# Expert weights in double tiles: 16 KB in a row on a partition where one is free, 8 KB otherwise

## The chip, the core and the metric

The kernel runs on one core of a Trainium2 chip. It is measured in microseconds (us) of device time for one execution; the median of three runs before the change is 1324.52 us (1322.39 to 1326.03). The engines are TensorE (PE; PEld is its weight load), VectorE (DVE), ScalarE (ACT), GpSimd (POOL) and SyncE (SP), which here issues nearly all loads. 16 DMA engines move the data; a packet is what one of them carries in one piece.

## The reference, cut to what matters

One layer of a diffusion model over 512 tokens of 1024 channels: adaLN modulation from a conditioning vector (`w_mod`), an input projection into attention, Hyena and Conformer branches, an output projection with a residual, and then 16 experts. Every expert takes the 64 tokens with the highest affinity. Everything is float32. What the change is about is the expert part:

```
aff = softmax(h @ w_router);  gate, idx = top_k(aff.T, 64)       # per expert
xe = h[idx]                                                     # 16 x 64 x 1024
a = einsum('ecd,edf->ecf', xe, w1);  u = einsum('ecd,edf->ecf', xe, w3)   # f: 2048
y = einsum('ecf,efd->ecd', silu(a) * u, w2) * gate
x = rmsnorm(x + g2 * zeros.at[idx].add(y), final_norm_g)
```

w1, w3 and w2 are 8 MB per expert each, 24 MB together and 384 MB for all 16. (MB here is 1,048,576 bytes.)

## The kernel before, in words

**Tiles.** Large data lies in 24 equal tiles of 128 partitions x 8 KB (1 MB each) of one pool: weights on their way, their split halves, activations, attention tables, the reloaded rows of x, the accumulator. `U` (L65) hands one out and counts it; `free` and `free_only` (L76, L80) take back a number of tiles, without naming them.

**Loads.** All loads are put into a list in the order of their use (L227 to L268) and are issued from SP. `pump(keep)` (L72) issues from the head of the list for as long as more than `keep` tiles are left by the count; `free` calls it. `take` (L166) hands over a loaded tile, and issues up to it where it isn't loaded yet. The keep values (`ADA_KEEP` L489, `PK` L734) hold tiles back for the work that comes next. A load waits on SP until its tile's last readers are done, and SP works through its queue in order. SP also waits for an earlier load of its own before it issues the next; some 8 are under way at a time.

**Channels.** An expert's w1 and w3 come in 8 blocks each of 128 rows (channels), one row of 8 KB per partition: block k holds channels 128k to 128k + 127. w2 comes in 8 blocks of 256 rows, two rows of 4 KB per partition. Each of these loads reads 1 MB that lies in one piece in memory. The activations must have the same channel on the same partition: x is transposed in blocks of 128 neighbouring columns (L1012, L1168, L1193), and the hidden activations are transposed for w2 with a column step of 2 (L1339), because a partition holds two neighbouring rows.

**Order of the work.** First filters, projections, convolution (to some 250 us), then attention and output projection with routing, in an order that is written out by hand for TensorE (L1103): S, T, A are steps of the attention, r the routing of a block of tokens, d a part of the last adaLN group (`adaln(3)`, four loads of `w_mod`), f the release of two tiles. `best` (L1077) finds the top tokens on DVE. Then comes the expert loop (L1300): for each of the 8 blocks it takes w1 and w3, runs 4 pairs of matmuls (L1313 and L1314, w1 and w3, each on one half of the array) and frees both tiles; every matmul shows as two in the records, so that a block has 8 pairs there. Between the blocks lie the scatter of the expert before (L1205, L1208) and the gather of the next one's rows (L1185, L1193). Then 16 transposes of the hidden activations (L1340), and 8 blocks of w2 with 4 pairs in the records each (L1353). After the last expert the accumulated rows are stored from SP (L1364), and the rows that the last expert changes are written again from POOL (L1381).

Of the kernel before, what the change touches and what calls it, by code (L numbers as in the profile page):

```python
# [25 lines left out]
NU = 24  # L26
# [24 lines left out]
def hybrid_kernel(ctx: ExitStack, tc: tile.TileContext, a, out: bass.AP):  # L51
    nc = tc.nc
    small = ctx.enter_context(tc.tile_pool(name="small", bufs=1))
    big = ctx.enter_context(tc.tile_pool(name="big", bufs=NU))
# [6 lines left out]
    used = [0]  # L61
    ready = {}
    limit = [12]

    def U(name, dt=FT):  # L65
        used[0] += 1
        assert used[0] <= NU, name
        return big.tile([128, 2048], dt, name=name, tag="U")
# [3 lines left out]
    def pump(keep=0):  # L72
        while loads and loads[0] is not None and used[0] < NU - keep and len(ready) < limit[0]:
            loads.popleft()()

    def free(k=1, keep=0):  # L76
        used[0] -= k
        pump(keep)

    def free_only(k=1):  # L80
        used[0] -= k
# [84 lines left out]
    def take(key):  # L166
        while key not in ready:
            assert loads and used[0] < NU, key
            go = loads.popleft()
            if go is not None:  # L170
                go()
        return ready.pop(key)
# [11 lines left out]
    def load_xr(i):  # L184
        def go():
            t = U("ld")
            for h in range(2):
                nc.sync.dma_start(t[:, h * D:(h + 1) * D], by_col(a["x"])[2 * i + h])
            ready["xr", i] = t
        loads.append(go)  # L190
# [61 lines left out]
    for u in (1, 0):  # L252
        for n in range(2):
            load(("wo", n, u), a["w_out"][u * 512:(u + 1) * 512, n * 512:(n + 1) * 512].rearrange("(k p) n -> p k n", p=128),
                 v512)
            if u and not n:
                load_xr(0)
                load_xr(1)
    for e in range(E):
        for k in range(8):  # L260
            if e == 0 and k == 6:
                for q in range(4):
                    load_wm(3, q)
            load(("w1", e, k), a["w1"][e, k * 128:(k + 1) * 128, :])
            load(("w3", e, k), a["w3"][e, k * 128:(k + 1) * 128, :])
        for j in range(8):

            load(("w2", e, j), a["w2"][e, j * 256:(j + 1) * 256].rearrange("(p k) n -> p (k n)", k=2))  # L268
# [46 lines left out]
    fw3s = [U("fw3s", FR) for _ in range(2)]  # L315
# [13 lines left out]
    free_only(1)  # L329
    xn = [take(("x", 0)), take(("x", 1))]  # L330
    ss = stat[:, 4:8]
    hr = [U("hr0"), U("hr1")]
# [16 lines left out]
    def x_transposed():  # L349
        yield from transpose_rows([half(xn[b // 2], b % 2) for b in range(4)], 4,  # L350
                                  lambda k4, b: v512(hr[k4]).rearrange("p k (c r) -> p k r c", r=8)[:, :, 2 * b:2 * b + 2])
        free_only(2)
# [3 lines left out]
    def filt_out():  # L356
        sd.extend([U("sm"), U("df")])
# [16 lines left out]
        free_only(4)  # L374
# [8 lines left out]
    def spectrum():  # L383

        sm, df = sd
        dft = v512(take("dft"))
        K.extend([U("KE"), U("KP"), U("KM")])
# [24 lines left out]
        free_only(3)  # L412


    def adaln(g):
# [10 lines left out]
        for k in range(8):  # L426
            if k % per == 0:
                w = take(("wm", g, k // per)).rearrange("p (k j n) -> p k j n", k=per, n=512)
# [3 lines left out]
            if k % per == per - 1:  # L432
                free_only(1)
                pump(ADA_KEEP[g])
                yield
# [16 lines left out]
        for blk in range(4):  # L452
            c = slice(blk * 128, (blk + 1) * 128)
            if ncol == 4:
                nc.tensor.transpose(p[:, c], row[:, c], ident)
# [33 lines left out]
    ADA_KEEP = [7, 4, 2, 0]  # L489
# [3 lines left out]

    def modulate_split(src, n, v, name, pool="01010101"):

        nu = (8 * n) // 2048
        hi = [U(name + "h", FR) for _ in range(nu)]
        lo = [U(name + "l", FR) for _ in range(nu)]
# [11 lines left out]
    def split(raw, keep, dve=()):  # L510
        hi = U("wh", FR)
        lo = U("wl", FR)
# [4 lines left out]
        free(1, keep)  # L517
# [26 lines left out]
    free_only(2)  # L544
# [9 lines left out]
    def mix_alloc(i):  # L554
        mixh[i] = U(f"mixh{i}", FR)
        mixl[i] = U(f"mixl{i}", FR)
# [8 lines left out]
    glt, yc = [], []  # L565
# [5 lines left out]
    def evac_cf(m, ps):  # L571
# [3 lines left out]
        else:  # L575
            if m == 0:

                glu = U("glu")
                glt.extend(glu[:, i * 544:i * 544 + 542] for i in range(2))
# [15 lines left out]
    def ln_cf():  # L595
# [27 lines left out]
        free_only(1)  # L623
# [6 lines left out]
    def evac_hy(i, ps):  # L630
        if i == 0:
            hx[0] = U("hx")
        if i == 4:
            hx[1] = U("hz")
# [8 lines left out]
    def hyena():  # L643
# [8 lines left out]
        for o in range(2):  # L652
# [59 lines left out]
            free_only(1)  # L712
        free_only(6)
# [7 lines left out]
    def evac_q(m, ps):  # L721
        if m == 0:
            Q.append(v512(U("Q")))
# [10 lines left out]
    PK = [6, 7, 3, 5, 8, 2]  # L734

    def project(c, ntile, evac, order=None, ctx_part=None):
# [5 lines left out]
        parts = []  # L742
# [734 lines left out]
```

## Time and profile before

| | |
|---|---|
| Median of 3 runs | 1324.52 us |
| Profiled execution, its time | 1322.8 us |
| Its span (first to last instruction) | 1321.0 us |
| PE busy | 1249.0 us (95%) |
| DVE, ACT, POOL busy | 39%, 17%, 12% |
| Moved by DMA | 457.99 MB (of 10^6 bytes), in 72979 packets |
| Expert loads | 384 of 1 MB, 19.9 us from issue to landing (median) |

The page divides the span into 40 slices of 33 us, and gives each engine's busy share there in tenths. The chain of waits goes back from the last instruction and names, at each step, what released it. Matmuls overlap in the records, so that a busy PE need not be at its peak, and a DMA share can come out a little above 1.

### The profile page before, as it was taken

To read this page: it belongs to the slowest core of one execution; us is meant where nothing else is said; L and a number is where in the kernel's file an instruction comes from. 1 tells how busy PE (TensorE), PEld (TensorE's weight loads), DVE (VectorE), ACT (ScalarE), POOL (GpSimd) and SP (SyncE) were. 2 spreads that over 40 slices of the span, in tenths; PEclk is the share of its full clock that TensorE was granted. 3 is DMA by queue.
4 is the path that set the end of the run, shared out by engine and by line. 5 is a ranking of instruction groups with operands and counts; after the bars stand their busy time and mean duration, and the time that the engine had idled before them with its cause. 6 is when DMAs were issued, how large, how long until landed. Compare 5 with 4: busy or idle time off the path is not lost.

```text
span 1321.0 us, 14776 instructions
## 1 busy us (share of the span) xinstructions
PE 1249.0 (95%) x5914; PEld 566.4 (43%) x5914; DVE 509.7 (39%) x1036; ACT 222.7 (17%) x478; POOL 157.1 (12%) x166
## 2 busy tenths in 40 slices
PE   6899989989989999999999999999999999999996
PEld 2577667866634333333333333333333333333332
DVE  6778998778670121212212123121211212121232
ACT  3542232345410010100101011010101001010111
POOL 2343444564210000000000000000000000000000
PEclk9999999999989999999999999999999999999999
DMA  9945026614489999999999999999999999999997
GB/s 346 384 165 185 32 68 181 227 25 160 144 366 376 420 419 420 420 420 419 419 419 419 419 419 420 418 420 420 420 420 419 420 420 420 420 420 420 419 419 300
DMA packets 72979, 457.99 MB, mean 347 GB/s; under 512 B 7364, under 2 KB 9228, under 8 KB 21710
## 3 DMA queue, kind: packets, MB, share of 16 engines
q1 hardware_dynamic: 71662, 453.64, 84.5%
q0 software_dynamic: 912, 3.06, 0.9%
q8 instruction: 46, 0.75, 0.2%
q10 hardware_dynamic: 336, 0.35, 0.1%
q14 instruction: 23, 0.19, 0.0%
HBM read 453.87 MB, written 2.36 MB: 345 GB/s over the span
## 4 chain that ended last, share of the span: by engine, by line
PE 48%; DMA 36%; DVE 12%; ACT 2%; issue 2%; POOL 0%; POOLq 0%; SPq 0%; ACTq 0%; DVEq 0%
DMA ld<-in_w_dram 35%; PE pa L1313 17%; PE py L1353 7%; DVE glu L590 4%; PE pZ L1205 3%; PE pG L1185 2%; PE pa L1314 1%; PE pS L932 1%; PE pP L550 1%; PE pO L963 1%; PE pP L549 1%; PE pP L548 1%; PE pT L1340 1%; DMA out_dram<-acc 1%; PE pX L548 1%
## 5 line engine op out<-in xcount | busy, mean ns | idle before, releaser
L1314 PE MATMUL pa<-ld,xh 128*64 128x512 f32 x1024 | 465.1, 599 | 11.5 <-DMA ld<-in_w_dram 11.5
L1313 PE MATMUL pa<-ld,xh 128*64 128x512 f32 x1024 | 467.2, 599 | 0.2 <-DVE xh L1065 0.2
L1313 PEld LDWEIGHTS pa<-ld,xh 128*64 128x64 f32 x1024 | 132.2, 137 | 217.4 <-issue 211.2
L1353 PE MATMUL py<-ld,xh 128*64 128x512 f32 x1024 | 224.5, 596 | 0.5 <-DMA ld<-in_w_dram 0.5
L1208 DVE TENSOR_TENSOR acc<-acc,pZ 128x512 f32<-128x512 f32 x112 | 73.2, 685 | 285.0 <-PE pZ L1205 284.6
L1314 PEld LDWEIGHTS pa<-ld,xh 128*64 128x64 f32 x1024 | 132.8, 137 | 84.0 <-issue 54.8
L1353 PEld LDWEIGHTS py<-ld,xh 128*64 128x64 f32 x1024 | 72.1, 138 | 141.3 <-issue 136.3
L1381 POOL DMA_INDIRECT out_dram<-yg,rwA x1 | 1.1, 1112 | 928.9 <-DVE yg L1380 928.9
L1063 ACT ACTIVATE xh<-pT,B,A 128x64 f32<-128x64 f32 (+1 forms) x60 | 24.3, 405 | 445.3 <-PE pT L1193 335.3
L1357 DVE SCALAR_TENSOR_TENSOR yg<-py,rwA,g1bc 128x512 f32<-128x512 f32 x16 | 12.0, 751 | 210.7 <-PE py L1353 210.7
L1205 PE MATMUL pZ<-yg,oh 64*128 64x512 f32 x240 | 83.2, 640 | 4.6 <-DVE acc L1208 3.9
L516 POOL TENSOR_TENSOR wl<-ld,wh 128x512 fp32r<-128x512 f32 x44 | 65.0, 1505 | 78.7 <-ACT wh L515 59.9
L548 PE MATMUL pP<-hh,wh 128*128 128x512 f32 x144 | 58.3, 406 | 1.2 <-ACT hh L505 1.2
L549 PE MATMUL pP<-hl,wh 128*128 128x512 f32 x144 | 57.5, 400 | 1.5 <-DVE hl L507 1.5
L550 PE MATMUL pP<-hh,wl 128*128 128x512 f32 x144 | 56.6, 399 | 1.1 <-DVE wl L516 1.1
L590 DVE SCALAR_TENSOR_TENSOR glu<-glu,p 128x512 f32<-128x512 f32 x60 | 55.3, 922 | 1.2
L1340 PE MATMUL pT<-c,au 128*128 128x128 f32 x256 | 49.4, 324 | 5.8 <-DVE xh L1343 2.2
L1185 PE MATMUL pG<-ld,ohg 128*64 128x512 f32 x224 | 52.5, 592 | 0.0
L103 ACT ACTIVATE xg<-pG 128x512 f32<-128x512 f32 x7 | 4.2, 597 | 274.6 <-PE pG L1185 274.6
L1205 PEld LDWEIGHTS pZ<-yg,oh 64*128 64x128 f32 x240 | 22.1, 184 | 64.7 <-issue 37.3
L1065 DVE TENSOR_SCALAR xh<-pT,A,B 128x64 f32<-128x64 f32 (+1 forms) x60 | 20.6, 344 | 74.9 <-ACT xh L1063 27.6
L1340 PEld LDWEIGHTS pT<-c,au 128*128 128x128 f32 x256 | 37.0, 210 | 26.9 <-DVE acc L1208 10.9
(343 smaller groups left out, 1347.8 us busy)
## 6 DMA issues: line engine op xcount, KB each, us to landing
ld<-in_w_dram SPq DMA_DIRECT2D x384, 1024.0 KB, 19.9
ld<-in_w_mod_dram SPq DMA_DIRECT2D x24, 1024.0 KB, 14.9
ld<-in_w_in_dram SPq DMA_DIRECT2D x11, 1024.0 KB, 7.3
ld<-in_w_out_dram SPq DMA_DIRECT2D x4, 1024.0 KB, 12.8
ld<-in_x_dram SPq DMA_DIRECT2D x2, 1024.0 KB, 12.6
ld<-in_x_dram SPq DMA_DIRECT2D x4, 512.0 KB, 6.9
out_dram<-acc SPq DMA_DIRECT2D x4, 512.0 KB, 16.8
g<-in_rpb_dram POOLq DMA_DIRECT2D x8, 244.5 KB, 4.0
```

Of the source, the lines that this page charges most:

```text
L516: (nc.vector if i in dve else nc.gpsimd).tensor_sub(lo[:, s], raw[:, s], hi[:, s].bitcast(FT))
L548: mm(ps, l[0], r[0], start=start, stop=False)
L549: mm(ps, l[0], r[1], start=False, stop=False)
L550: return mm(ps, l[1], r[0], start=False, stop=stop)
L590: nc.vector.scalar_tensor_tensor(yc[i], glt[i][:, j:j + 512], cw[:, i, j:j + 1], yc[i], op0=OP.mult, op1=OP.add)
L1185: mm(pg[64 * h:64 * h + 64], g[:, 64 * b:64 * b + 64], xblk(b)[:, 512 * h:512 * h + 512], start=(b == 0), stop=(b == 3))
L1205: mm(ps[h], oh[pr, 128 * c:128 * c + 128], yg[pr], start=True, stop=True)
L1208: nc.vector.tensor_add(ablk(c)[:, s], (ablk if e else xblk)(c)[:, s], ps[h])
L1313: mm(pa[f][0:64], xT[:, k, cs], w1[:, s], start=(k == 0), stop=(k == 7))
L1314: mm(pa[f][64:128], xT[:, k, cs], w3[:, s], start=(k == 0), stop=(k == 7))
L1340: nc.tensor.transpose(p[:, i * 128:(i + 1) * 128], au[f][:, c:c + 255:2], ident)
L1353: mm(py[64 * h:64 * h + 64], hT[:, f], w2[:, i * 1024 + 512 * h:i * 1024 + 512 * h + 512], start=(f == 0), stop=(f == 15))
```

## The change

The pool of 24 tiles becomes 8 single tiles of 8 KB and 8 double tiles of 16 KB per partition. Where two tiles of work belong together (`U2`), they are the halves of a double if one is free. A tile is freed by name now; a double is free again when both halves are. A half may serve a single tile of the same type when its partner is not in use (`halves`).

An expert load (`load_expert`) covers two of the old blocks: if a double is free, one transfer of 2 MB with 16 KB in a row on each partition; otherwise two transfers of 1 MB, each of which reads every second 8 KB out of the same stretch. So that both forms put the same channel on the same partition, a partition holds two neighbouring rows of w1 and w3, and block k is every second channel out of 256 (`alternate`); for w2 it is four neighbouring rows, and the transposes of the hidden activations have a step of 4. The transposes of x, its gathers, the modulation vectors, the router's rows and the norm's gain follow that order. Four keep values are higher, and `free(6, 4)` after the projections has keep 7. The list has w1 and w3 in pairs: w1 of blocks 0 and 1, w3 of blocks 0 and 1, and so on. The reload of x is one step with four transfers.

```diff
-NU = 24
+NS, ND = 8, 8
...
     def U(name, dt=FT):
+        if single[0] < NS:
+            single[0] += 1
+            t = big.tile([128, 2048], dt, name=name, tag="U", bufs=NS)
+            held[id(t)] = t, None
+            return t
+        if not halves[dt]:
+            assert double[0] < ND, name
+            halves[dt].append(pair_of(name, dt)[1])
+            both = held[id(halves[dt][0])][1]
+            both[0] -= 1
+            return both[1]
+        t = halves[dt].pop()
+        held[id(t)][1][0] += 1
+        return t
+
+    def pair_of(name, dt=FT):
+        double[0] += 1
+        d = big.tile([128, 4096], dt, name=name, tag="D", bufs=ND)
+        two = [d[:, 0:2048], d[:, 2048:4096]]
...
+    def U2(name, dt=FT):
+        return pair_of(name, dt) if double[0] < ND else [U(name, dt) for _ in range(2)]
...
+    def free_only(*tiles):
+        for t in tiles:
+            both = held.pop(id(t))[1]
+            if both is None:
+                single[0] -= 1
+                continue
+            both[0] -= 1
+            if not both[0]:
+                double[0] -= 1
...
+    def load_expert(w, e, q):
+        n = 512 if w == "w2" else 256
+        src = a[w][e, n * q:n * (q + 1)]
+        at = [0]
+
+        def of_expert(keep):
+            if at[0] == 0 and double[0] < ND and left() >= keep + 2:
+                two = pair_of("ld")
+                nc.sync.dma_start(held[id(two[0])][1][2], src.rearrange("(p k) n -> p (k n)", k=n // 128))
+                ready[w, e, 2 * q], ready[w, e, 2 * q + 1] = two
+                at[0] = 2
+            elif single[0] < NS and left() > keep or halves[FT] or double[0] < ND and left() >= keep + 2:
+                t = U("ld")
+                nc.sync.dma_start(t, src.rearrange("(p h k) n -> h p (k n)", h=2, k=n // 256)[at[0]])
+                ready[w, e, 2 * q + at[0]] = t
+                at[0] += 1
...
+    alternate = lambda k: slice(256 * (k // 2) + k % 2, 256 * (k // 2) + k % 2 + 255, 2)
...
-    ADA_KEEP = [7, 4, 2, 0]
+    ADA_KEEP = [7, 5, 3, 0]
...
-    PK = [6, 7, 3, 5, 8, 2]
+    PK = [6, 7, 3, 5, 8, 3]
...
-            nc.tensor.transpose(p[:, 128 * c:128 * c + 128], xg[:, 128 * c:128 * c + 128], ident)
+            nc.tensor.transpose(p[:, 128 * c:128 * c + 128], xg[:, alternate(c)], ident)
...
-                acc = [U("acc0"), U("acc1")]
+                acc = U2("acc")
...
-                c = 256 * (i // 2) + i % 2
-                nc.tensor.transpose(p[:, i * 128:(i + 1) * 128], au[f][:, c:c + 255:2], ident)
+                nc.tensor.transpose(p[:, i * 128:(i + 1) * 128], au[f][:, i:i + 509:4], ident)
```

## Rows read from the trace of the kernel before

**Rows 1.** The page's 40 slices: busy tenths, DMA share, GB/s.
```profile
PE   6899989989989999999999999999999999999996
...
DMA  9945026614489999999999999999999999999997
GB/s 346 384 165 185 32 68 181 227 25 160 144 366 376 420 419 420 420 420 419 419 419 419 419 419 420 418 420 420 420 420 419 420 420 420 420 420 420 419 419 300
```

**Rows 2.** Chain of waits in time, 400 to 1321 us: start, length, what.
```profile
433.64 14.65 PE py L1353 x64
...
712.79 13.88 PE py L1353 x64
...
767.86 13.88 PE py L1353 x64
...
797.21 20.48 DMA ld<-in_w_dram
```

**Rows 3.** SP's waits, 400 to 1321 us: total, times, longest.
```profile
SPq L162 <- DMA ld<-in_w_dram: 583.1, 280, 3.1
SPq L162 <- PE pa L1314: 105.7, 48, 6.0
SPq L162 <- PE py L1353: 63.6, 40, 7.2
```

**Rows 4.** Windows by row length: length, PE busy, clock, DMA share, GB/s.
```profile
216.00:224.00 8.00, 5.67 (x27) 1.00 1.03 224
224.00:228.00 4.00, 4.00 (x31) 1.00 1.05 384
348.00:354.00 6.00, 5.73 (x53) 1.00 0.98 393
...
440.00:1200.00 760.00, 741.31 (x3260) 1.00 1.01 420
```

**Rows 5.** The same view where expert 0 begins.
```profile
390.00:395.00 5.00, 4.82 (x17) 0.58 0.43 177
395.00:400.00 5.00, 5.00 (x30) 1.00 0.35 102
...
410.00:420.00 10.00, 10.00 (x52) 1.00 0.97 388
```

**Rows 6.** Groups by shape, PEld and ACT: busy us, mean ns, idle before.
```profile
L1340 PEld LDWEIGHTS pT<-c,au 128*128 128x128 f32 x256 | 37.0, 210 | 26.9 <-DVE acc L1208 10.9 <-DVE xh L1343 10.4 <-ACT xh L1063 2.3
...
L1193 PEld LDWEIGHTS pT<-c,xg 128*128 128x128 f32 x56 | 5.9, 141 | 11.4 <-issue 11.4
...
L636 ACT ACTIVATE u<-pP 128x512 f32<-128x512 f32 x6 | 6.6, 1098 | 11.1 <-PE pP L550 9.3 <-DVE hx L641 1.7
...
L103 ACT ACTIVATE xg<-pG 128x512 f32<-128x512 f32 x7 | 4.2, 597 | 274.6 <-PE pG L1185 274.6
```

**Rows 7.** Timeline of one expert's transposes: start, length, instruction.
```profile
655.24 0.56 PEld L1340 LDWEIGHTS pT<-c,au 128*128 128x128 f32 x4 [0.29 <-DVE acc L1208]
...
656.06 0.56 PEld L1340 LDWEIGHTS pT<-c,au 128*128 128x128 f32 x4 [0.27 <-DVE xh L1343]
```

**Rows 8.** Timeline, w2 matmuls of the last expert.
```profile
1296.78 12.37 PE L1353 MATMUL py<-ld,xh 128*64 128x512 f32 x56
...
1309.61 1.94 PE L1353 MATMUL py<-ld,xh 128*64 128x512 f32 x8 [0.47 <-DMA ld<-in_w_dram]
```

**Rows 9.** Timeline, the last adaLN group: its loads on SP, its matmuls, routing.
```profile
346.55 14.50 SPq L162 DMA_DIRECT2D ld<-in_w_mod_dram  x4
...
369.83 1.04 PE L431 MATMUL pM<-ld,sc 128*2 128x512 f32 x8
...
372.09 1.04 PE L431 MATMUL pM<-ld,sc 128*2 128x512 f32 x8
...
374.44 0.27 PE L1056 MATMUL pR<-c,lg 128*16 128x128 f32 x1 [1.31 <-DVE lg L1053]
374.64 1.90 PE L431 MATMUL pM<-ld,sc 128*2 128x512 f32 x16
```

More of the change, by code (lines that the diff above doesn't have):

```diff
@@ L59, in hybrid_kernel, with left @@
     early = until_routed.enter_context(tc.tile_pool(name="early", bufs=1))
[L61 removed]
+    single = [0]
+    double = [0]
+    halves = {FT: [], FR: []}
+    held = {}
     ready = {}
     limit = [12]
+    def left():
+        return 2 * (ND - double[0]) + NS - single[0]
     def U(name, dt=FT):
[L66 to L68 removed]
+        if single[0] < NS:
[12 more added lines that the diff above has]
+        return t
@@ L70, in hybrid_kernel @@
+    def pair_of(name, dt=FT):
+        double[0] += 1
+        d = big.tile([128, 4096], dt, name=name, tag="D", bufs=ND)
+        two = [d[:, 0:2048], d[:, 2048:4096]]
+        both = [2, two[0], d]
+        for t in two:
+            held[id(t)] = t, both
+        return two
+    def U2(name, dt=FT):
+        return pair_of(name, dt) if double[0] < ND else [U(name, dt) for _ in range(2)]
     loads = deque()
     def pump(keep=0):
-        while loads and loads[0] is not None and used[0] < NU - keep and len(ready) < limit[0]:
-            loads.popleft()()
@@ L76, in free @@
-    def free(k=1, keep=0):
-        used[0] -= k
+        while loads and loads[0] is not None and len(ready) < limit[0]:
+            if loads[0].__name__ == "of_expert":
+                if not loads[0](keep):
+                    return
+            elif single[0] < NS and left() > keep or halves[FT] or double[0] < ND and left() >= keep + 2:
+                loads.popleft()()
+            else:
+                return
+    def free_only(*tiles):
[7 more added lines that the diff above has]
+                double[0] -= 1
+                for h in halves.values():
+                    h[:] = [x for x in h if held[id(x)][1] is not both]
@@ L78, in free @@
+    def free(*tiles, keep=0):
+        free_only(*tiles)
         pump(keep)
-    def free_only(k=1):
-        used[0] -= k
     def psA(name="psA"):
@@ L167, in take @@
         while key not in ready:
[L168 to L171, printed above, removed]
+            assert loads, key
+            if loads[0] is None:
+                loads.popleft()
+            elif loads[0].__name__ == "of_expert":
+                assert loads[0](0), key
+            else:
+                loads.popleft()()
         return ready.pop(key)
@@ L182, in hybrid_kernel, with load_xr @@
     by_col = lambda t: t.rearrange("(r b c) d -> b c r d", r=8, c=16)
[L184 to L190, printed above, removed]
+    def load_xr():
+        t = U2("ld")
+        for h in range(4):
+            nc.sync.dma_start(t[h // 2][:, (h % 2) * D:(h % 2 + 1) * D], by_col(a["x"])[h])
+        ready["xr"] = t
+    def load_expert(w, e, q):
[8 more added lines that the diff above has]
+                at[0] = 2
+            elif single[0] < NS and left() > keep or halves[FT] or double[0] < ND and left() >= keep + 2:
+                t = U("ld")
+                nc.sync.dma_start(t, src.rearrange("(p h k) n -> h p (k n)", h=2, k=n // 256)[at[0]])
+                ready[w, e, 2 * q + at[0]] = t
+                at[0] += 1
+            else:
+                return False
+            if at[0] == 2:
+                loads.popleft()
+            return True
+        loads.append(of_expert)
     v512 = lambda t: t.rearrange("p (k n) -> p k n", n=512)
@@ L256, in hybrid_kernel @@
             if u and not n:
-                load_xr(0)
-                load_xr(1)
+                loads.append(load_xr)
     for e in range(E):
[L260 to L268, printed above, removed]
+        for q in range(4):
+            if e == 0 and q == 3:
+                for k in range(4):
+                    load_wm(3, k)
+            for w in ("w1", "w3"):
+                load_expert(w, e, q)
+        for j in range(4):
+            load_expert("w2", e, j)
     def norm_rows(rows, junk, n, ss, rs):
```

126 lines of the change are left out of this document (65 added, 61 removed).

## The prediction

> **What bounds the kernel now.** I read the share of the DMA engines by slice first. From about a third of the span to the end they are busy without a break at 418 to 420 GB/s, and TensorE is busy too [rows 1]; two engines at 9 in every slice don't say which one is the limit. The chain of waits in order of time settles it: until 797 us it runs over TensorE, one expert every 55.07 us (712.79 to 767.86), and from 797 us over expert loads, some 20 us each from issue to landing [rows 2]. One expert is 24 loads of 1 MB (a tile of 8 KB on 128 partitions); at 420 GB/s [rows 4] a load takes 1.0486/0.42 = 2.497 us, and an expert 59.9 us. So TensorE, 4.9 us quicker per expert, eats a stock that was loaded ahead, and when the stock is gone, the queue sets the pace up to the end. The DMA queue's own waits say the same: 583 us for an earlier load of its own, 169 us for TensorE to release a tile [rows 3]. The end of the kernel therefore is: the time at which the stream begins, plus the bytes that are left then, by the rate, plus a tail. The change touches all four.
>
> **The rate.** How long one packet holds an engine can be read at three row lengths; I divide the rate by the share, since shares run a little over 1. Rows of 8 KB: 420/1.01 = 415.8 GB/s, so 16 x 8192 B / 415.8 = 315.2 ns. Rows of 4 KB (w_mod): 393/0.98 = 401.0, 163.4 ns. Rows of 2 KB (w_out): 384/1.05 = 365.7, 89.6 ns [rows 4]. From 4 to 8 KB a packet grows by 151.8 ns, so 11.6 ns of it don't go with its length; from 2 to 4 KB the same sum gives 15.8 ns. One packet of 16 KB would then take 315.2 + 303.6 = 618.8 ns in place of 630.4: 1.84% less. Bounds: 0, if 16 KB still goes as two packets; 2.5% with 15.8 ns. No row of 16 KB is in the trace, so 1.84% is an extrapolation.
>
> Not every load gets it. I followed the new rules for single and double tiles through the whole program, tile by tile: of 384 MB of expert weights 131 loads are of 2 MB and 122 of 1 MB. After the first expert's first release 364 MB remain, 252 of them (69%) in long rows. The rest keep 8 KB packets, now every second 8 KB of a stretch; w_mod, whose rows are cut out of rows of 24 KB, lies on the line of the other two lengths [rows 4], so I see no loss in that. Before, 364 MB is 364 x 2.497 = 909 us; 0.69 x 1.84% = 1.27% of it is **-11.5 us** (0 to -15.7).
>
> The Trainium skill (DMA: Bandwidth & Descriptors, Why small descriptors are slow) puts the fixed cost of a packet at about 3 cycles, and calls joining worthwhile only up to 256 B. For 8 KB, 256 beats of 32 B, that is an estimate of 3/259, half of which goes: 0.58%, -3.6 us in place of -11.5. The rows above speak for three times that; by the page the whole sum would end slower than before.
>
> **The start of the stream.** Before, 22 MB of experts are in tiles when expert 0 begins, and the queue pauses, all tiles full: its share falls to 0.43 and 0.35 between 390 and 400 us, and up to 420 us the rate is still at 388 GB/s [rows 5]. By the new rules only 20 MB are in, because a double is free again only when both halves are; two consumed halves stand idle. That is 2 x 2.497 = +5.0 us. Against it: of the four w_mod loads of the last adaLN part, the third and fourth get their tile only when the first and second are consumed. Before, the four are issued from 346.6 to 361 us and consumed from 369.8 on [rows 9]. Issued one by one behind the first and the second group of matmuls, at 371 and 373 us, they hold up all that is behind them in SP's order: 8 MB, which then run from 378 to about 398 us and so fill the old pause and its dip, worth some 2 us. I take **+3 us** (0 to +6). The last two adaLN groups end some 3.5 us later; the last routing step on TensorE (L1056) lies ahead of them [rows 9], so what waits is adaLN's own gain, which is needed only when expert 0 ends.
>
> **The tail.** Before, the last w3 tile holds up one block of 8 pairs of matmuls. After, the last w3 load is a double, and two blocks can start only when it has landed: 8 pairs more at 13.88/32 = 0.434 us [rows 2], +3.5 us. Then come 16 transposes whose stationary operand is now read with a step of 4 elements. With step 2 their weight load takes 210 ns, with step 1 141 ns [rows 6]. Step 4 isn't in the trace. The nearest row is ACT's evacuation with a step of 8, 1098 ns against 597 ns [rows 6]; if the load doubles likewise, a group of four, which comes every 0.82 us (655.24, 656.06) with 0.56 us of loads [rows 7], takes about 0.3 us more: +1.2 us per expert. The bounds are 0 and, with a tripled load, +3.4 us. In the last expert TensorE waited 0.47 us for the last w2 tile, and the 64 matmuls ended at 1311.55 and not at 1296.78 + 13.88 = 1310.66 [rows 2, 8]; that 0.9 us was DMA, and covers as much. Together 3.5 + 1.2 - 0.9 = **+3.8 us** (+1 to +7). The stores of the output stand in the same queue behind the loads, and gain with them.
>
> **What costs nothing.** The stride in every other expert (1.2 us, and 4 transposes of xg with step 2, 0.1 us): TensorE then takes 56.4 us per expert, the DMA 59.9 x 0.9873 = 59.1. The cover is 2.7 us; without it each further us per expert is 15 us. The x_rows and first_rows blocks with step 2 (about 70 ns per load, some 8 in the path of the routing): 0.3 us. Fewer issues: SP waits anyway. Tighter keep values and pairs in the first 240 us move about a dozen loads to a later release, none of them by more than the slack that I see, since DVE's convolution is the chain there; but w_mod parts come just ahead of use: +0.2 us (-2 to +4).
>
> Sum: -11.5 + 3 + 3.8 + 0.5 = -4.2 us. The profiled execution took 1322.8 us (span 1321.0), 1.7 below the median of the runs shown, 1324.5: so 1318.6 there, and **1320 us** as a median.
>
> **Rivals.**
> 1. The rate doesn't change: 16 KB goes as two packets, or what is fixed is not the packet's. Against it stands that three lengths fit one line. Costs alone: 3 + 3.8 + 0.5 = +7.3 us, 1332. By the skill's 3 cycles the sum would be +3.7, 1328.
> 2. TensorE becomes the bound. Place: the step-4 weight loads between the two halves of every expert, 16 each. Price: with the tripled load 3.4 us, 58.5 us per expert. From expert 0's end at 448.3 us [rows 2] TensorE alone would end its last matmul at 448.3 + 2 + 15 x 58.5 = 1328 us, against 1311.55 [rows 8]: +16, 1341. It decides from about +2.1 us per expert, where TensorE's own end passes that of the stream. The Trainium skill (SBUF — State Buffer, the note on cachelines under the port swizzle) says that reads want two hits per line of 16 bytes: 4 fp32 elements apart is one hit. No row here has that step on TensorE; with step 2, two hits, the load is already 69 ns longer [rows 6], so the trace doesn't bear the rule out as it stands.
> 3. The start and the tail cost nothing: the queue's order leaves no deficit of 2 MB and TensorE catches up at the end. Then -11.5, 1313.
> 4. The 16 engines read addresses twice as far apart and collide. One pattern of this trace, the reload of x with rows far apart, ran at 224 GB/s with a share of 1.03 [rows 4]. On 252 MB: 252 x 2.497 x 0.875 = +551 us. The x reload also spreads its partitions otherwise, and w_mod's pitch of 24 KB does no harm, so I hold this to be unlikely.
>
> **How the numbers follow.** Forecast 0.45 (its own range 1315 to 1326), rival 1 0.15, rival 2 0.13, rival 3 0.24, rival 4 0.03. What a measurement of this kernel tells from no change is about 0.3%, 4 us: faster is below 1320.5. Half of the forecast and all of rival 3 lie there, 0.48; within 4 us lie nearly half of the forecast and some of rival 1, 0.25; slower 0.27. The range, 1309 to 1335, takes in the forecast, rival 3 and rival 1; rivals 2 and 4 are left out.
>
> **What would show it.** Packets fall from 72,979 by 131 x 128 = 16,768 (rival 1: they don't), and the rate in the long stretch rises to about 425. The chain passes from TensorE to the DMA later than 797 us, near 1100 (rival 2: never, and the weight loads of the au transposes are above 300 ns). At 395 us the stock is 2 MB lower, with a break between 362 and 378. TensorE's last block of w1/w3 takes 6.9 us after the last landing. I am wrong if the rate stays at 420, if TensorE's period per expert passes 57.2 us, or if expert 0 begins later than before.

## The result, and the profile after

The changed kernel takes 1336.32 us (median of 5 runs, 1333.97 to 1338.42) beside 1325.02 us for the kernel before on the same chip (1322.39 to 1326.92): ratio 1.0085, 95% interval 1.0064 to 1.0106. It is slower by 0.9%, some 11 us; 1320 was forecast, with a range of 1309 to 1335. The profiled execution took 1333.97 us, its span 1332.2 us, 11.2 longer than before.

The stream itself does what was forecast. First two lines of the page, then windows (length; busy time of PE, PEld, DVE, ACT and POOL with the number of their instructions; clock, DMA share, GB/s):

```profile
GB/s 351 344 155 173 80 64 170 129 56 173 128 347 306 423 424 423 426 424 424 428 424 422 426 423 425 426 425 425 424 425 423 424 426 424 426 426 424 425 424 238
DMA packets 54113, 457.96 MB, mean 344 GB/s; under 512 B 5268, under 2 KB 7132, under 8 KB 19614
```

```profile
360.00:370.00 10.00, 9.75 (x101) 7.71 (x100) 5.27 (x18) 4.41 (x13) 2.36 (x10) 1.00 0.21 58
370.00:380.00 10.00, 8.86 (x67) 5.97 (x65) 9.60 (x41) 3.20 (x9) 2.67 (x10) 1.00 1.01 411
...
400.00:410.00 10.00, 9.27 (x42) 5.41 (x42) 3.14 (x14) 1.05 (x2) 0.00 (x0) 0.70 0.22 93
410.00:420.00 10.00, 10.00 (x54) 4.42 (x52) 0.41 (x1) 0.46 (x1) 0.00 (x0) 1.00 0.89 357
440.00:1200.00 760.00, 740.90 (x3252) 259.66 (x3250) 158.63 (x325) 61.10 (x143) 0.00 (x0) 0.99 1.01 425
```

425 GB/s in place of 420 at the same share. But two holes stand ahead of it: 58 GB/s from 360 to 370 us and 93 from 400 to 410, where before's stream had 333 and 411. Summed over windows of 10 us from the start of the span to 420 us, the changed stream is 7.0 MB (10^6 bytes), some 16.5 us, behind. By 1300 us it has made good 4.4 MB of that, 10.3 us.

In the second hole all tiles are full: from 404 to 408 us next to nothing moves, until expert 0 gives tiles back. So the first hole is made good by then, and what counts is when expert 0 starts. The chain of waits (start, length, what) leads to its first matmul, the last line, at 404.49 us; before it began at 390.62:

```profile
377.94 0.97 PE pM L505 x8
...
380.20 1.02 PE pM L505 x8
...
381.24 15.67 DMA ld<-in_w_mod_dram
...
396.95 1.08 PE pM L505 x8
...
398.06 0.60 ACT mrow L510
...
398.71 1.61 PE pB L517 x4
...
400.32 1.05 PE pB L1237 x4
...
401.86 2.08 PE pT L1247 x8
...
404.49 1.09 PE pa L1392
```

TensorE works in order. Its matmuls on the third and fourth w_mod tiles (L505), and the spreading of their result (pB L517), stand ahead of the gather of expert 0's rows (pB L1237, pT L1247). The fourth load takes 15.67 us, but most of that runs beside the routing's top-k on VectorE. What it costs is read between the routing's result (p) and the first use of the gather's pB (ohg). VectorE's timeline before, and after:

```profile
386.47 0.28 DVE L1151 TENSOR_TENSOR p<-g1bc,lists 16x128 f32<-16x128 f32 x1
387.57 1.37 DVE L1161 TENSOR_SCALAR ohg<-pB,c,stat 128x128 f32<-128x128 f32 x4 [0.83 <-PE pB L1158]
```

```profile
394.46 0.28 DVE L1230 TENSOR_TENSOR p<-g1bc,lists 16x128 f32<-16x128 f32 x1
401.40 1.37 DVE L1240 TENSOR_SCALAR ohg<-pB,c,stat 128x128 f32<-128x128 f32 x4 [6.66 <-PE pB L1237]
```

1.1 us became 6.9. SP's timeline shows why the loads come late; it answers to the first line of [rows 9], where all four were issued from 346.55 us:

```profile
368.15 0.89 SPq L208 DMA_DIRECT2D ld<-in_w_mod_dram  x2
372.10 3.79 SPq L248 DMA_DIRECT2D ld<-in_w_dram  x3
378.98 2.64 SPq L208 DMA_DIRECT2D ld<-in_w_mod_dram  x2
395.57 2.83 SPq L253 DMA_DIRECT2D ld<-in_w_dram  x2
```

The list has the four w_mod loads together, behind the third pair of w1 and w3 of expert 0. In SP's queue three loads of 2 MB (L248), which come later in the list, now stand ahead of the last two w_mod, and the fourth lands behind them.

That is 5.9 of the 13.9 us; the other 8.0 were lost before: the routing's result p is that much later. The first score matmul (pS L1011) begins at 262.4 us (256.7 before), the third block of scores at 277.8 (266.6): 5.7 us late, then 11.2. By the sixteenth block, 352.9 against 345.0, 3.3 are regained. The step from 5.7 to 11.2 is one late w_out load. The timeline of all engines in the changed kernel, and SP's of the kernel before:

```profile
262.81 0.37 SPq L208 DMA_DIRECT2D ld<-in_w_out_dram  x1
...
268.20 2.49 DVE L946 TENSOR_TENSOR ld<-ld,g1bc 128x512 f32<-128x512 f32 x4 [2.27 <-DMA ld<-in_w_out_dram]
...
271.82 0.66 PE L1031 MATMUL pT<-c,P 128*128 128x128 f32 x4 [3.69 <-DVE P L1024]
```

```profile
127.44 45.21 SPq L162 DMA_DIRECT2D ld<-in_w_in_dram  x3
...
214.70 28.60 SPq L162 DMA_DIRECT2D ld<-in_w_out_dram  x3
```

Before, the last w_out load was issued by 243.3 us (214.70 + 28.60). After, it gets its tile at 262.81; VectorE, in order too, stops at the multiplication by g1 (L946) with the scores' scaling behind it, and TensorE stops for that. Likewise the last w_in loads come from 158 to 188 us (127 to 173 before). It is the double tiles that hold these loads back: with 24 single tiles and the same keep values (e5 below) they come as early as before:

```profile
125.70 45.22 SPq L208 DMA_DIRECT2D ld<-in_w_in_dram  x3
...
211.54 32.59 SPq L208 DMA_DIRECT2D ld<-in_w_out_dram  x3
```

Behind expert 0's start little is different. The chain passes to the DMA at 776.76 us (797.21 in [rows 2], and near 1100 was forecast). The weight loads by shape, for [rows 6], and the last expert's w2 matmuls, for [rows 8]:

```profile
L1416 PEld LDWEIGHTS pT<-c,au 128*128 128x128 f32 x256 | 37.9, 211 | 26.9 <-DVE xh L1419 10.6 <-issue 5.3 <-ACT xh L1142 5.3
...
L1272 PEld LDWEIGHTS pT<-c,xg 128*128 128x128 f32 x56 | 7.8, 209 | 11.4 <-issue 11.4
```

```profile
1308.79 7.09 PE L1429 MATMUL py<-ld,xh 128*64 128x512 f32 x32
1315.71 1.89 PE L1429 MATMUL py<-fg,xh 128*64 128x512 f32 x8
1317.43 5.32 PE L1429 MATMUL py<-ld,xh 128*64 128x512 f32 x24
```

Step 4 costs 211 ns, step 2 209 to 210. The matmuls end at 1322.75 us, 11.2 later than the 1311.55 before; from expert 0's start that is 918.3 us against 920.9.

### The profile page after: what moved, and what is told of

It reads as the page before. It is cut to its first block, busy times and chain, and to the rows that moved or that the text cites. A ratio compares the mean times of both kernels' runs of the same rounds, so it can differ in the third digit from the quotient of the medians.

```text
span 1332.2 us, 14504 instructions
## 1 busy us (share of the span) xinstructions
PE 1251.2 (94%) x5914; PEld 561.7 (42%) x5914; DVE 500.9 (38%) x1036; ACT 223.6 (17%) x478; POOL 154.2 (12%) x166
## 4 chain that ended last, share of the span: by engine, by line
PE 46%; DMA 35%; DVE 14%; issue 2%; ACT 2%; POOL 1%; POOLq 0%; SPq 0%; DVEq 0%; ACTq 0%
DMA ld<-in_w_dram 30%; PE pa L1392 17%; PE py L1429 7%; DVE glu L667 4%; PE pZ L1284 3%; DMA ld<-in_w_mod_dram 2%; PE pG L1264 2%; PE pa L1393 2%; DMA out_dram<-acc 1%; PE pT L1416 1%; PE pO L1042 1%; DVE t L762 1%; PE pS L1011 1%; PE pP L626 1%; PE pP L627 1%
## 5 line engine op out<-in xcount | busy, mean ns | idle before, releaser
L1393 PE MATMUL pa<-ld,xh 128*64 128x512 f32 x1016 | 458.2, 596 | 4.8 <-DMA ld<-in_w_dram 4.7
L1392 PE MATMUL pa<-ld,xh 128*64 128x512 f32 x1016 | 460.9, 597 | 0.0
L593 POOL TENSOR_TENSOR w<-ld,w 128x512 fp32r<-128x512 f32 x42 | 61.5, 1487 | 86.4 <-ACT w L592 86.4
L626 PE MATMUL pP<-hl,w 128*128 128x512 f32 x144 | 57.4, 399 | 3.1 <-DVE hl L585 3.1
L625 PE MATMUL pP<-hh,w 128*128 128x512 f32 x144 | 57.9, 404 | 1.2 <-ACT hh L583 1.2
L627 PE MATMUL pP<-hh,w 128*128 128x512 f32 x144 | 56.3, 397 | 2.5 <-DVE w L593 2.5
L1264 PE MATMUL pG<-ld,ohg 128*64 128x512 f32 x224 | 55.5, 592 | 0.0
## 6 DMA issues: line engine op xcount, KB each, us to landing
ld<-in_x_dram SPq DMA_DIRECT2D x2, 1024.0 KB, 12.4
```

Of the source, the lines that this page charges most:

```text
L593: (nc.vector if i in dve else nc.gpsimd).tensor_sub(lo[:, s], raw[:, s], hi[:, s].bitcast(FT))
L625: mm(ps, l[0], r[0], start=start, stop=False)
L626: mm(ps, l[0], r[1], start=False, stop=False)
L627: return mm(ps, l[1], r[0], start=False, stop=stop)
L1264: mm(pg[64 * h:64 * h + 64], g[:, 64 * b:64 * b + 64], xblk(b)[:, 512 * h:512 * h + 512], start=(b == 0), stop=(b == 3))
L1392: mm(pa[f][0:64], xT[:, k, cs], w1[:, s], start=(k == 0), stop=(k == 7))
```

## The experiments

T is the theory under test throughout: the time is the start of expert 0 plus a stretch that the change hardly alters, and the start is late because of loads ahead of it, not because of the rows or the tail. The table has, for each kernel, the start of expert 0 and the rest of the span from there (us, of its profiled execution), the rate from 440 to 1200 us (GB/s), and the median, with the ratio to the kernel before (interval) of paired runs.

```
                         start   rest   GB/s  median   ratio
before                   390.6   930.4  420   1325.02
the change               404.5   927.7  425   1336.32  1.0085 (1.0064-1.0106)
e1  w_mod before q 2     401.1   929.7  425   1332.26  1.0062 (1.0041-1.0084)
e2  w_mod before q 1     400.6   929.3  425   1331.62  1.0057 (1.0034-1.0079)
e3  rows of 8 KB         408.5   934.6  420   1343.47  1.0147 (1.0124-1.0171)
e4  step 2               404.4   929.9  425   1336.38  (one run)
e5  24 singles           398.1   933.5  419   1333.98  1.0073 (1.0054-1.0091)
e6  16 + 4               402.2   933.7  422   1341.17  1.0131 (1.0112-1.0150)
e7  12 + 6               406.8   931.9  423   1337.22  1.0089 (1.0068-1.0111)
e8  10 + 7               401.7   929.1  422   1337.44  1.0102 (1.0083-1.0121)
e9  24 singles, keep 4   390.5   931.8  419   1325.89  1.0016 (1.0006-1.0026)
e10 24 singles, ScalarE  385.7   933.6  419   1324.12  0.9998 (0.9988-1.0007)
e11 halves reused        408.4   933.0  423   1342.75  1.0141 (1.0124-1.0157)
e12 the same, ScalarE    397.9   933.1  423   1332.87  1.0068 (1.0056-1.0081)
e13 e1, ScalarE          396.6   929.7  425   1330.60  1.0052 (1.0037-1.0068)
e14 e13, last w1/w3      400.9   927.8  425   1330.72  1.0050 (1.0031-1.0068)
e15 12 + 6, ScalarE      392.7   929.2  423   1325.46  1.0013 (1.0001-1.0024)
e16 16 + 4, ScalarE      391.8   934.8  422   1328.75  1.0040 (1.0025-1.0055)
e17 before, ScalarE      389.2   930.9  420   1321.61  0.9992 (0.9982-1.0001)
e18 before, delayed      406.4   928.3  420   1336.77  1.0099 (1.0079-1.0120)
```

Over all twenty the start varies by 22.8 us, the rest by 7.1. (e14 is the program of e13 up to its last expert, so a start is good to some 4 us between executions.)

**e1, e2: the w_mod loads earlier in the list.**

```diff
-            if e == 0 and q == 3:
+            if e == 0 and q == 2:      # e2: q == 1
```

> The changed kernel with the four loads of the last adaLN part one place earlier in the list of loads (ahead of the third pair of w1 and w3 of expert 0 instead of the fourth), so that all four get a tile in one go. Theory T (expert 0 begins late because the fourth w_mod load queues behind 6 MB of experts, and TensorE's order holds the routing behind it): the first expert matmul returns from 404.5 to 390-393 us, the pause of the queue at 400-410 us goes, and the time falls from 1336 to 1322-1327 (13.9 us if TensorE's start decides, about 10 if only the pause of the stream is won back). Rival U (the start was absorbed; the doubles' waiting or the tail cost the 11 us): expert 0 may begin earlier, but the time stays at 1333-1338.

> As before, but two places earlier (ahead of the second pair of w1 and w3), so that the w_mod loads are issued some 10 us sooner and the first expert tiles later. Theory T: the same first expert matmul as in the first run within 2 us, 1321-1328; what counts is only that the fourth w_mod tile has landed before about 375 us. Rival U: 1333-1338. A third possibility: the expert loads pushed back are missed, and the time is 3 us or more above that of the first run.

In e1 all four w_mod loads are issued in one go (in e2 one at 308 us and the others by 358):

```profile
356.49 14.98 SPq L208 DMA_DIRECT2D ld<-in_w_mod_dram  x4
```

From the routing's result to the gather it is 1.1 us again. VectorE's timeline in e1:

```profile
396.91 0.28 DVE L1230 TENSOR_TENSOR p<-g1bc,lists 16x128 f32<-16x128 f32 x1
398.00 1.37 DVE L1240 TENSOR_SCALAR ohg<-pB,c,stat 128x128 f32<-128x128 f32 x4 [0.81 <-PE pB L1237]
```

So the cause of the 5.9 us is shown. But both kernels are only 3 to 5 us quicker than the change, with intervals that overlap its own, and both expectations of the time were missed: the routing, 8.0 us late in the change, is 10.4 and 9.8 late in these two executions, and it is what expert 0 now waits for. The larger part of the loss sits elsewhere.

**e3: the doubles as two loads with rows of 8 KB; e4: the transposes with step 2 (its values differ).**

```diff
-                nc.sync.dma_start(held[id(two[0])][1][2], src.rearrange("(p k) n -> p (k n)", k=n // 128))
+                for h in range(2): nc.sync.dma_start(two[h], src.rearrange("(p h k) n -> h p (k n)", h=2, k=n // 256)[h])
...
-                nc.tensor.transpose(p[:, i * 128:(i + 1) * 128], au[f][:, i:i + 509:4], ident)
+                nc.tensor.transpose(p[:, i * 128:(i + 1) * 128], au[f][:, 256 * (i // 2) + i % 2:256 * (i // 2) + i % 2 + 255:2], ident)
```

> The changed kernel with every 2 MB load of a double tile issued as two loads of 1 MB, each of 8 KB rows into its half: same tiles, same layout, same order. Theory T: packets return to some 71,000-73,000, the rate in the long stretch falls from 425 to 420 GB/s, the first expert matmul stays at 404.5 us within 1, and the end comes 6 to 11 us later: 1342-1347. Rival R (the rate rose for another reason, such as fewer issues or the layout of the tiles, or the rate isn't what sets the end): within 3 us of 1336.

> The changed kernel with the transposes of au read with a step of 2 elements again instead of 4 (the hidden features meet the rows of w2 in another order, so the values of the experts differ; nothing else is changed). Theory T: the step costs nothing; weight loads of 210 ns as with step 4, TensorE 55.9-56.7 us per expert as in the changed kernel, its 16 transposes 3.3 us. Rival S (step 4 is what made TensorE 0.7 us per expert slower than in the kernel before): 55.1 us per expert.

e3 has 72,978 packets again and this window:

```profile
440.00:1200.00 760.00, 738.73 (x3227) 254.73 (x3225) 156.75 (x320) 60.00 (x140) 0.00 (x0) 0.99 1.01 420
```

So the long rows make 425 of 420 GB/s. From 440 to 1300 us that is 4.3 MB, 10.2 us. In the time, e3 is 7.2 us slower than the change by the medians (1343.47 against 1336.32) and 8 by the ratios, but expert 0 also began 4.0 us later, which the expectation excluded. From expert 0 on the difference is 6.9 us: the last load of e3 lands 10.5 us later against expert 0's start, and the last matmul ends 3.3 us after it in place of 6.8. So the tail takes back some 3.6 us of what the long rows give. In e4 the weight load is 212 ns and TensorE takes 55.9 to 56.9 us per expert (55.9 to 56.7 after): the step costs nothing. What TensorE's period grew by (55.07 in [rows 2]) is mostly a wait of the scatter for VectorE's accumulation (some 0.7 us per expert), and it is there at either step.

**e5 to e8: other mixes of tiles.** Only the line `NS, ND = 8, 8` is edited: 24, 0; 16, 4; 12, 6; 10, 7.

> The changed kernel with 24 single tiles and no double: channels taken alternately, pairs in the list of loads and step-4 transposes all stay, every load is 1 MB with 8 KB rows. Theory T2 (the 14 us by which expert 0 begins late come from double tiles that are free only as a whole: 8 us before the routing ends, 6 us for the fourth w_mod load; the rate and the tail make up the rest): first expert matmul at 390-392 us, 420 GB/s, 1322-1327. Rival L (the new order of the list or the layout of the channels costs something by itself): 1328 or more, with expert 0 or TensorE's 16 transposes late.

> 16 single tiles and 4 doubles: 76 loads of 2 MB, 40% of the expert bytes (68% in the changed kernel), and in the order of the loads the w_out loads stand ahead of all experts and the four w_mod loads in one go, as before. Theory T2: first expert matmul at 390-393 us; the rate gains 0.4/0.68 of the measured 7 to 10 us, so 4 to 6 us; up to 4 us of tail and stock against it: 1318-1325. Rival V (it is doubles in the expert phase, not in the early phase, that cost the time): 1326-1332.

> 12 single tiles and 6 doubles: 95 loads of 2 MB, 49% of the expert bytes; w_out loads and the four w_mod loads stand in the order as with 16 and 4. Theory T2: first expert matmul at 390-394 us; the rate gains 5 to 7 us: 1317-1325. Rival V: 1328-1334.

> 10 single tiles and 7 doubles: the first expert load stands ahead of nothing of w_out any more, but the fourth w_mod load stands behind 6 MB of expert loads again. Theory T2: expert 0 begins 4 us or more later than with 12 and 6, and the time is above that one's by as much, 1324-1332. Rival V: no step here, only a slow rise with the number of doubles.

e5 to e7 went against me, and in e8 expert 0 begins 5.1 us earlier than in e7 where 4 us later was expected. In e5, with 24 single tiles, the loads come early again and the scores begin nearly in time (first block 257.5 us, third 267.4, both 0.8 later than before). So both early losses come from the double tiles. Yet expert 0 starts 7.4 us later than before. The loss is one instruction in the timeline of all engines:

```profile
282.47 1.28 POOL L593 TENSOR_TENSOR w<-ld,w 128x512 fp32r<-128x512 f32 x1
282.65 9.82 DVE L1024 TENSOR_SCALAR P<-P,m 128x512 f32<-128x512 f32 x1
...
283.69 1.27 POOL L993 TENSOR_TENSOR ld<-ld,t 128x512 f32<-128x512 f32 x1
...
284.92 3.69 POOL L593 TENSOR_TENSOR w<-ld,w 128x512 fp32r<-128x512 f32 x3
288.57 4.51 POOL L927 TENSOR_TENSOR tm<-c,g 128x256 f32<-128x256 f32 x6
...
292.57 0.81 DVE L1024 TENSOR_SCALAR P<-P,m 128x512 f32<-128x512 f32 x1
...
292.61 0.66 PE L1031 MATMUL pT<-c,P 128*128 128x128 f32 x2 [7.68 <-DVE m L1023]
```

The scaling of the scores P, from SBUF to SBUF, normally takes 0.48 us. Here it lasts 9.82, until ten of GpSimd's eleven instructions without a gap are through, and TensorE waits 7.68 us for it. e6 and e7 have the same (10.19 us at 275.30, 9.82 at 291.11); e8 and the change itself have no scaling that long. New theory K: the two engines keep each other out, and a GpSimd run without gaps keeps VectorE out for all of it. The order on these engines isn't written by hand, and shifts with the releases and keep values. Rival: the scaling waits for something that the trace doesn't name.

**e9, e10, e15, e16: K, with the order of before, or with the scaling on another engine.** e9 has 24 singles with keep 4 after the projections, which gives VectorE and GpSimd the order of the kernel before. e10 is e5 with:

```diff
-            nc.vector.tensor_scalar(p, p, m2[:, 2:3], None, op0=OP.mult)
+            nc.scalar.activation(p, p, AF.Copy, scale=m2[:, 2:3])
```

e15 is e7 with it, e16 is 16 + 4 tiles with it and keep 4.

> 24 single tiles as in the fifth run, and one number more taken back: after the k projection 4 tiles are kept for later allocations, as in the kernel before, not 7. With that the order of GpSimd's, VectorE's and ScalarE's instructions in the attention is that of the kernel before. Theory K (the order of the work ahead of expert 0 is what cost the fifth run its 9 us: there one VectorE instruction, the scaling of P, took 9.82 us in place of 0.49, while ten GpSimd instructions ran without a gap): first expert matmul at 390-392 us, 1323-1327. Rival L (alternate channels, the list of loads or the step-4 transposes cost something by themselves): 1330 or more still.

> 24 single tiles as in the fifth run with its order of GpSimd's instructions untouched, but the scaling of P (32 instructions) is done by ScalarE in place of VectorE. Theory K2 (GpSimd's run of instructions locks VectorE out of SBUF, and that is what held up TensorE): no wait of 8 us between the sixth and the seventh block of scores (5 to 7 us from one to the next, 14.7 us in the fifth run), first expert matmul at 390-394 us, 1323-1329. Rival O (the late blocks waited for what GpSimd computes, not for VectorE): the gap stays over 12 us and the time at 1332-1336.

> As the seventh run (12 singles, 6 doubles) with the scaling of P on ScalarE and nothing else. There one VectorE instruction took 9.82 us at 291 us. Theory K2: the instruction is gone from VectorE, expert 0 begins 8 to 13 us earlier than in the seventh run (406.8), at 394-399, and the time falls from 1337 to 1325-1330. Rival O: 1334-1338.

> As the sixth run (16 singles, 4 doubles), with 4 tiles kept after the k projection as in the kernel before, and the scaling of P on ScalarE. Theory K2 with W: expert 0 at 388-395 us in place of 402.2; at 40% of the bytes in 16 KB rows the rate gives 4 to 5 us, of which the tail takes 2 to 3 back: 1320-1326, at best a few us below the kernel before. Rival O: 1332 or more.

e9 starts at 390.5 us, 7.6 earlier than e5, and is some 2 us slower than the kernel before (at most 3.4 by its interval). As its list still has the pairs, alternate channels and step 4, these cost no more than that. In e10 GpSimd runs the same instructions as closely, and VectorE goes on beside it:

```profile
282.01 3.77 POOL L593 TENSOR_TENSOR w<-ld,w 128x512 fp32r<-128x512 f32 x3
...
282.64 0.69 DVE L1019 CUSTOM_DVE_ANT_1 P<-pS,tm 128x512 f32<-128x512 f32 x1
...
283.26 0.69 DVE L1019 CUSTOM_DVE_ANT_1 P<-pS,tm 128x512 f32<-128x512 f32 x1
...
284.30 0.69 DVE L151 COPY PT<-pT 128x512 f32<-128x512 f32 x1
...
285.28 1.32 ACT L1024 ACTIVATE P<-P,m 128x512 f32<-128x512 f32 x2
...
285.75 4.42 POOL L927 TENSOR_TENSOR tm<-c,g 128x256 f32<-128x256 f32 x6
```

On ScalarE the scaling (L1024) takes 0.66 us beside the same run. The start is 12.4 us earlier than e5's, the time 9.9 us less. That is more than the one lock: the start is also 4.9 us ahead of the kernel before, and what the other 31 scalings, or VectorE's shorter list of work, have of it was not told apart. e15 is 10 to 12 us quicker than e7 (by the ratios, by the medians) with the same one line, and so the best kernel with double tiles: 0.1% from the kernel before, and not faster. e16 stops short of it: its rest is 934.8 us, with TensorE waiting 2.28 us for loads in the last expert. K holds, the rival falls: what is kept out is the 128x512 instruction from SBUF to SBUF, while those with an operand in PSUM (pS, pT above) go on.

**e11, e12: 8 + 8 tiles, a freed half may be used again at once (and w_mod as in e1).** e12 has the scaling on ScalarE too.

```diff
+            if both[0]:
+                if limit[0] < 99:
+                    halves[both[3]].append(t)
```

> The changed kernel with 8 and 8 tiles, but a consumed half of a double tile may be taken again for a load of 1 MB until the routing, and the last adaLN part's loads stand one place earlier. The w_out loads then stand ahead of all experts again, and 82 loads in place of 131 are of 2 MB. Theory T3 (the loads ahead of expert 0 got their tiles late because half-consumed doubles stood idle; w_in at 188 us in place of 173, w_out at 263 in place of 243): w_in and w_out loads as early as before within 5 us, expert 0 at 391-396 us unless VectorE is locked out as in the fifth run; the rate gains 0.43/0.68 of the changed kernel's: 1320-1328. Rival O: expert 0 at 400 us or later though the loads come early, 1330-1336.

> As the eleventh run, with the scaling of P on ScalarE as in the tenth. Theories T3 and K2 together: expert 0 at 388-394 us, and with the gain of the rate 1318-1325, no slower than the kernel before. Rival O: no gain over the eleventh run, 1330-1336.

All w_out loads are ahead of the experts again (228.61 to 254.65 us in e12) and the gap of 11.4 us between the second and third block of scores (266.4 to 277.8 after) shrinks to 7.1. But e11 runs into the same lock (9.82 us at 294.02), and only 82 loads are of 2 MB: slower. e12 takes 9.9 us off that, but begins expert 0 at 397.9 us, not the 388 to 394 expected. So the late w_out load is mended by free tiles; the idea doesn't pay.

**e13, e14: e1 with the scaling on ScalarE; in e14 the last w1 and w3 doubles of the last expert as two halves.**

> The first run's kernel (8 and 8 tiles, w_mod loads in time) with the scaling of P on ScalarE. In the first run expert 0 began at 401.1 us, 10.5 late, without a VectorE instruction of 10 us in its trace. Theory P (what is left of the lateness is loads that come late and VectorE's order ahead of the attention; the lock adds only single instructions of 1.5 us): about the 5 us that the scaling on ScalarE gave with 24 tiles between the first and last block of scores: expert 0 at 395-398 us, 1326-1330. Theory W (at 8 and 8 the doubles pay 3 to 4 us as soon as expert 0 begins no later than 393): only if it does, 1318-1322. Rival N: no gain, 1331-1334.

> As the thirteenth run, and the last doubles of w1 and w3 of the last expert are loaded as halves of 1 MB with 8 KB rows, one after the other. Theory Q (the end is TensorE's: a double of w3 lets two blocks wait for one landing, some 5 us after the last load instead of 2): 2 to 4 us below the thirteenth run, TensorE's last expert matmul 4 to 5 us after the last w2 load lands. Rival S (TensorE no longer waits for a load in the last expert, so the halves change nothing): within 1 us of it.

e13 gains little over e1 (1 to 2 us, with overlapping intervals): at 8 + 8 the lock is not the main loss, the late w_out load is still there (266.3 to 276.7 between those blocks). e14 changes nothing: the tail isn't set by the last double of w3.

**e17, e18: the kernel before, with the scaling on ScalarE; and with expert 0 delayed.** e18 adds, ahead of expert 0:

```diff
+    for _ in range(16):
+        mm(pw, ident, xblk(0)[:, 0:512], start=True, stop=True)
```

> The kernel before with the scaling of P on ScalarE and nothing else. T (VectorE is kept out by GpSimd while the scores are scaled, and that can cost some 5 us ahead of expert 0): expert 0 begins 0 to 5 us earlier than 390.6 us, and as the queue then pauses with all tiles full, at most some 2 us of it reach the end: 1321 to 1324, ratio 0.998 to 1.000. Rival (ScalarE, which has the exponentials to do in that stretch, becomes the chain): expert 0 at 392 us or later and 1326 or more.

> The kernel before with 16 extra matmuls of 128x512 (about 14 us, results not used) on TensorE just ahead of expert 0; loads, list and tiles as before. T (when the stock is full the stream stops until expert 0 gives tiles back, so a late start alone moves the end): expert 0 at about 404 us, as in the changed kernel; the stream uses some 2 to 3 us of the delay to fill what was not yet full; 1335 to 1338, ratio 1.008 to 1.011. Rival (TensorE is 4.9 us quicker per expert than the stream and makes a late start good; the loss of the changed kernel is in its loads): 1324 to 1327.

The timeline of TensorE and two windows of e18:

```profile
390.52 15.93 PE L1233 MATMUL pw<-ld,c 128*128 128x512 f32 x32
406.38 0.64 PE L1315 MATMUL pa<-ld,xh 128*64 128x512 f32 x1
```

```profile
390.00:400.00 10.00, 10.00 (x22) 4.56 (x21) 1.78 (x10) 0.00 (x0) 0.00 (x0) 0.78 0.24 97
400.00:410.00 10.00, 10.00 (x36) 4.31 (x36) 0.00 (x0) 0.46 (x1) 0.00 (x0) 1.00 0.01 2
```

A start 15.8 us late, with nothing else touched, costs 14.0 us (1336.77 against 1322.73): all tiles are full and the queue stands at 2 GB/s until expert 0 gives tiles back. So a late start alone is enough to move the end by nearly as much, and the 13.9 us of the change are enough for its 11. The missing 2 us are the part of the delay in which the stream fills what was not yet full. e17 is the quickest kernel of all, 1321.61 us, but its interval, 0.9982 to 1.0001, doesn't exclude no change; in the kernel before the lock cost little.

## Why the prediction was wrong

**What bounds the kernel, the rate: right.** A stream that sets the end from the moment when it can begin is what e18 shows. The rate came out as forecast, 425, with 131 loads of 2 MB; packets fell by 18,866 (16,768 was worked out for the expert loads alone, and packets under 512 B fell by 2,096). The term, -11.5 us, measured -10.2 as bytes of the stream (440 to 1300 us, against e3), so it was right to some 10%; what reached the end in e3 was 7 to 8, with the tail against it. The Trainium skill (DMA: Bandwidth & Descriptors, Why small descriptors are slow) gives 3 cycles per packet and no use in joining beyond 256 B. An estimate from that figure made the term -3.6 us. Here doubling rows of 8 KB in 69% of the bytes gave 1.2% of rate, so the measurement decides against it.

**The start of the stream: right in its own terms.** I had +5.0 us for 2 MB less in tiles and some -2 for the pause and its dip. With all tiles full the changed stream stands at 73.4 MB (404 to 408 us) and e18's, with the old tiles, at 75.5 (404 to 410): 2.1 MB less, 5.0 us. And e18 lost 14.0 us by a start 15.8 late. So +3 is about what was measured. Not right was the order: three loads of 2 MB went ahead of the last two w_mod loads, which I had holding up all that is behind them.

**When expert 0 begins: the step that failed.** I had the start of expert 0 where it was, with +0.2 us for all loads ahead of it; it began 13.9 us late. Two sentences failed. The dozen loads moved "to a later release, none of them by more than the slack that I see": I had looked at VectorE's convolution as the chain, and not at the last w_out load, which came 19.5 us later (243.3 to 262.8) and stopped VectorE and then TensorE; 8.0 us were lost by the first top-k (360.0 to 368.0 us). And "what waits is adaLN's own gain, which is needed only when expert 0 ends": I had followed the data and not TensorE's order, in which the matmuls and the spreading of that gain stand ahead of expert 0's gather (the chain above); 5.9 us. I had put the routing's last step ahead of it, but not what comes behind. The sign that I named for being wrong, expert 0 later than before, is the one that came.

**The tail: size near, reason not shown.** +3.8 was forecast; the last matmul ends 6.8 us after the last landing (1315.9), 2.0 before: +4.9. But TensorE's last wait for a load is 0.25 us at 1227 us, none is in the last expert, and e14, which takes the last w1/w3 doubles away, moved neither the time nor the 6.8 (6.9). So the double of w3 is not the reason. The 2 MB loads have a part in it, as e3, with the same tiles and loads of 1 MB, has 3.3; which of them was not tested.

**The rest.** Step 4: 211 ns where I took 0.3 us more per group; +1.2 was 0. TensorE's period, 55.9 to 56.7 us, met my 56.4 by accident, from a wait in the scatter. From expert 0 on, the rate (-10.2), the tail (+4.9), the stock (+5.0) and the dip (some -2) make -2.3; -2.7 was measured. With the 13.9 us of the start that is the 11.2 us of the span. So the other terms were near, and the start of expert 0 is nearly the whole error. The chain, though, passes to the DMA at 777 us and not near 1100; why was not looked into.

**The rivals.** 1 (rate unchanged) and 4 (collision) fall with 425 GB/s, 2 (step 4) with 211 ns. The Trainium skill (SBUF — State Buffer, the note on cachelines) would make step 4 dearer than step 2; the two are equal here. 3 had no cost in the start, and missed by 23 us. 1336 lies between the times of 1 (1332) and 2 (1341), by neither's mechanism. None of my rivals was late routing, or a queue order that TensorE has to wait behind; that was the case that came.

**What stays open.** 5.7 us were lost before the first scores, and the double tiles cause them (e5); by which way is open: the w_in loads (31 us later to begin) go with it, but e12, which mends w_out, has them late too and was not split further, and VectorE's shift of work among its convolution was not told apart from them. Why e6 and e8 measure 3 to 5 us more than their profiled executions was not looked into. Single executions of one program differ by some 4 us in the start, so smaller differences between starts in the table tell nothing. The tail's reason is open as said.

## What to carry to other kernels

When a stream runs into full tiles, look for what holds the first consumer before you look at the rate: 15.8 us there were 14.0 at the end in e18, and 1.2% of rate had to pay for 14 of them here. For each load that a new allocation makes later, ask which in-order engine has its consumer, and what stands behind that consumer in the order, not only who needs its data. A change in tile sizes also reshuffles the engines' order; compare the durations of single instructions with their usual ones, since the 0.48 us instruction that took 9.8 here was a lock between two engines, and not what the mix of tiles was meant to change.

## What the runs showed of the hardware

- A scaling of 128x512 from SBUF to SBUF on VectorE (0.48 us) lasted 9.82 us in e5, e7 and e11 and 10.19 in e6 while GpSimd ran without a gap. In the kernel before a two-input operation of 1.6 us took 5.75 beside such a run of 5.03 us. The Trainium skill (SBUF — State Buffer, Who interferes with whom) says that the two share a port pair, held for a whole instruction; the trace agrees that one waits for the other, but here the loser waited through ten instructions, not one.
- Rows of 16 KB on a partition in 69% of the bytes: 425 GB/s, rows of 8 KB: 420 (e3), same share (1.01).
- TensorE's transposes load their weights in 141 ns at step 1, 210 at step 2, 211 at step 4.
